# Linear attention beside weight products: the update of a pair's second state moved into the step that retrieves the next pair, its scaled keys and masked queries made a step ahead

## The chip, the cores and the metric

The program is one launch on one core of a Trainium2 chip. The metric is the time of that launch on the device in microseconds; for the kernel before, the median of three runs is given. Times inside the launch come from one further, profiled execution, and count from the start of its span.

## The reference, cut to what matters

One inference step of one decoder layer for a prompt of 256 tokens and for 8 sample sequences of 8 tokens. Everything is float32. The layer is feed-forward, token mixing, feed-forward; the token mixing has, beside an attention branch, a linear attention with a matrix state, 4 heads of 256 x 256 for each sample. For each sample and head it computes:

```
num   = wgt @ v + sc * (q @ C0)          # retrieval: queries on the old state
C_new = sT * C0 + sum_s e_s k_s v_s^T    # the state's update, an output
```

C0 is an input (8 samples x 4 heads x 256 KB) and C_new is an output of the same size. All 320 tokens (256 of the prompt, 64 of the samples) run through the same weight matrices.

## The kernel before, in words

The weight products take nearly all of TensorE's time. A float32 product is made of three matmuls in a rounded 32-bit format: weights and inputs are each split in a high and a low part. `run_job` goes through the weight matrices in chunks of 512 KB. For a chunk, SyncE issues the load into a tile `raw` (5 buffers), ScalarE makes the high part `hi` by a cast (L225), VectorE makes the low part `lo` by a subtraction (L226), three chunks ahead of their use (3 buffers each), and TensorE runs 24 matmuls into a PSUM tile `fg`.

All other work is written as Python generators ("background"), which `run_job` advances by one step between chunks; what a step issues stands in each engine's queue ahead of the chunk's matmuls, and behind the casts for the chunk three further on. There are lists `every`, `slow` (sample attention, 8 steps in 15 chunks), `even` and `odd`; a generator on `odd` gets one step every second chunk. The linear attention, `mlstm` (L995), is on `odd`. All loads and stores are issued by SyncE in one order, the order of the program. Each waits there for what it needs, and everything behind it waits with it. `later(fn, n)` puts a store at the start of the chunk n chunks on.

In `mlstm`, head h works through its 8 sample states in four pairs s4 = 0..3: the states of samples s4 and s4+4. Each pair takes two steps, here called A and B:

- Step A: `retrieve` (L1132), four matmuls of the masked queries `qm` on the two state tiles `C`; `state(h, s4)` (L1146), two matmuls of the scaled keys `ks` with the values `vs` into a PSUM tile `bg`, one VectorE operation that adds them to the state tile (L1153), and its store; `make_ks(h, s4 + 4)` (L1042), two ScalarE operations (L1047, L1048) and one on GpSimd (L1049). For s4 = 0 of the heads 1 to 3 also `rms_out(h - 1)` (L1200), three VectorE operations (L1202, L1204) and the store `hm_d<-hh`.
- Step B: `state(h, s4 + 4)`; `make_ks(h, s4 + 1)` and `make_qm(h, s4 + 1)` (two GpSimd operations, L1038) for the next pair; `load_cc`, two loads of 256 KB, for the pair after the next; and, for s4 = 2, `load_head(h + 1)`.

After the four pairs come `numer` (the prompt's part, and `load_vals`, the loads `vh<-vm_d` for the next head), `rms_in`, and a step with `rms_sum` and `update(h + 1)`, whose first matmuls read `vh`, and which loads the next head's second pair.

A state tile is one of nine buffers of the tag `m2`, shared with the head's other tiles. `ks` has two buffers, `qm` one, `bg` four, of which the retrieval holds one through the head.

Of the kernel before, what the change touches and what calls it, by code (L numbers as in the profile page):

```python
# [128 lines left out]
def decoder_kernel(tc, I, O, K):  # L129
# [10 lines left out]
    def dma(out, in_):  # L140
        nc.sync.dma_start(out, in_)

    def mm(out, a, b, start=True, stop=True, **kw):
        T.matmul(out, a, b, start=start, stop=stop, **kw)  # L144

    def bcast(ap, n, at=1):
        shape = list(ap.shape)
        shape.insert(at, n)
        idx = [slice(None)] * len(ap.shape)
        idx.insert(at, None)  # L150
        return ap[tuple(idx)].to_broadcast(shape)
# [6 lines left out]
    def later(fn, n=1):  # L158
        later_q.append([n, fn])
# [94 lines left out]
    def bg_tile():  # L254
        return pp.tile([128, 512], F32, tag="bg", bufs=4, name="bg")
# [119 lines left out]
    state = {}  # L375
# [135 lines left out]
    def mxt(shape, tag, bufs, name, dt=F32):  # L511
        return M["p"].tile(shape, dt, tag=tag, bufs=bufs, name=name)
# [407 lines left out]
    def qk_evac(ps, j):  # L920
# [35 lines left out]
        if M["qk"] == 2:  # L956
            spawn(mlstm(), odd)
# [37 lines left out]
    def mlstm():  # L995
# [12 lines left out]
        Cq = [None]  # L1008

        def load_head(h):  # L1010
            q, k, re = mp_tile("q"), mp_tile("k"), mp_tile("re")
            dma(q, qk_d[h].rearrange("p (a n) -> p a n", a=2))
            dma(k, qk_d[4 + h].rearrange("p (a n) -> p a n", a=2))
            dma(re, raw_ap(rows_d[:], h * 2 * NT, [[0, 128], [NT, 2], [1, NT]]))
            scb = mxt([128, 2 * NS], "scb", 1, "scb")
            dma(scb, sc_d[h:h + 1].to_broadcast([128, 2 * NS]))
            vq = m2_tile("vq")
            for g in range(2):
                dma(vq[:, g * 256:(g + 1) * 256], raw_ap(vm_d[:], (SEQ + 32 * g) * 1024 + h * 256,
                                                        [[0, 4], [1024, 32], [1, 256]]))  # L1020
            H[h] = {"q": q, "k": k, "re": re, "scb": scb, "vq": vq}

        def load_vals(h):
            v = m3_full("vh")
            G.memset(v[:, 0:2, 256:257], 1.0)
            dma(v[:, 0:2, 0:256], vm_d[0:SEQ, h * 256:(h + 1) * 256].rearrange("(t p) c -> p t c", p=128))
            dma(v[:, 2, 0:256], vm_d[NT - 128:NT, h * 256:(h + 1) * 256])
            H[h]["v"] = v

        def load_c(b, h):  # L1030
            t = m2_tile("C")
            dma(t.rearrange("p (k v) -> p k v", k=2), C0d[b, h].rearrange("(k p) v -> p k v", p=128))
            return t

        def make_qm(h, s4):
            qm = mxt([128, 2, 2, 32], "qm", 1, "qm")
            for kt in range(2):
                G.tensor_tensor(qm[:, kt], H[h]["qsc"][:, kt].rearrange("p (g c) -> p g c", g=2), bcast(qmk[:, s4], 2),  # L1038
                                op=OP.mult)
            H[h]["qm"] = qm  # L1040

        def make_ks(h, b):  # L1042
            d = H[h]
            ks = mxt([128, 256], "ks", 2, "ks", F32R)
            x, e = d["kr"][:, (b // 4) * 256:(b // 4 + 1) * 256], d["eb"][:, b:b + 1]
            kf = mxt([128, 256], "kf", 1, "kf")
            S.activation(ks, x, AF.Copy, scale=e)  # L1047
            S.activation(kf[64:128], x[64:128], AF.Copy, scale=e[64:128])  # L1048
            G.tensor_tensor(ks[64:128], kf[64:128], ks[64:128].bitcast(F32), op=OP.subtract)  # L1049
            d["ks"] = ks  # L1050

        def prep(h):
            d = H[h]
# [78 lines left out]
        def retrieve(h, s4):  # L1132
            d = H[h]
            if s4 == 0:
                d["ip"] = bg_tile()
            ip, qm = d["ip"], d["qm"]
            for kt in range(2):
                for n in range(2):
                    x = 32 * (kt * 2 + n)
                    mm(ip[x:x + 32, 0:256], qm[:, kt, n], Cq[0][n][:, kt * 256:(kt + 1) * 256], s4 == 0, s4 == 3,  # L1140
                       tile_position=(0, x))
            if s4 == 3:
                d["isb"] = mxt([128, 256], "isb", 1, "isb")
                S.copy(d["isb"], ip[:, 0:256])

        def state(h, b):  # L1146
            d = H[h]
            ks, vs_, t = d["ks"], d["vs"], Cq[0][b // 4]
            cu = bg_tile()
            for kt in range(2):  # L1150
                mm(cu[:, kt * 256:(kt + 1) * 256], ks[:, kt * 128:(kt + 1) * 128],
                   vs_[:, (b // 4) * 256:(b // 4 + 1) * 256])
            V.scalar_tensor_tensor(t, t, sTb[:, h * 8 + b:h * 8 + b + 1], cu, op0=OP.mult, op1=OP.add)  # L1153
            later(lambda: dma(C1d[b, h].rearrange("(k p) v -> p k v", p=128), t.rearrange("p (k v) -> p k v", k=2)))

        def numer(h):
            d = H[h]
            z, v, qn, re, isb = (d[x] for x in ("z", "v", "qn", "re", "isb"))
            A, B = bg_tile(), bg_tile()
            mm(B[:, 0:256], ones, z[:, 0:256], True, False)  # L1160
            mm(B[:, 128:256], ones, z[:, 256:384], False, True)
            mm(B[:, 256:320], ones, z[:, 384:448], True, False)
            mm(B[:, 256:320], ones, qn[:, 0], False, True)
            for vt in range(2):
                vs = slice(vt * 128, (vt + 1) * 128)
                o = vt * 256
                mm(A[:, o:o + 256], v[:, 0, vs], z[:, 0:256], True, False)
                mm(A[:, o + 128:o + 256], v[:, 1, vs], z[:, 256:384], False, True)
                c = 320 + 64 * vt
                mm(B[:, c:c + 64], v[:, 2, vs], z[:, 384:448], True, False)  # L1170
                mm(B[:, c:c + 64], isb[:, vs], sels, False, True)
            rd = re[:, 0]
            V.tensor_scalar(rd, B[:, 0:NT], -1.0, None, op0=OP.mult)
            V.tensor_tensor(rd, rd, B[:, 0:NT], op=OP.max)
            hh = mp_tile("hh")
            S.copy(hh[:, :, 0:SEQ], A.rearrange("p (a n) -> p a n", a=2))
            S.copy(hh[:, :, SEQ:NT], B[:, 320:448].rearrange("p (a n) -> p a n", a=2))
            V.tensor_tensor(rd, rd, re[:, 1], op=OP.max)
            V.reciprocal(rd, rd)
            V.tensor_tensor(hh, hh, bcast(rd, 2), op=OP.mult)  # L1180
            d["hh"] = hh
# [18 lines left out]
        def rms_out(h):  # L1200
            hh, rs, sg = (H[h][x] for x in ("hh", "rs", "sg"))
            V.tensor_tensor(hh, hh, bcast(rs, 2), op=OP.mult)  # L1202
            for m in range(2):
                V.scalar_tensor_tensor(hh[:, m], hh[:, m], gv[:, G_MN + 2 * h + m:G_MN + 2 * h + m + 1], sg[:, m],  # L1204
                                       op0=OP.mult, op1=OP.mult)
            later(lambda: dma(hm_d[h].rearrange("p (a n) -> p a n", a=2), hh), 2)

        seq = [(h, s4) for h in range(4) for s4 in range(4)]
        CC = {}

        def load_cc(i):
            if i < 16:
                h, s4 = seq[i]
                CC[i] = [load_c(s4, h), load_c(s4 + 4, h)]
# [12 lines left out]
        update(0)  # L1227
        load_cc(1)
        for h in range(4):
            for s4 in range(4):  # L1230
                yield
                Cq[0] = CC.pop(4 * h + s4)
                retrieve(h, s4)
                state(h, s4)
                make_ks(h, s4 + 4)
                if s4 == 0 and h:
                    rms_out(h - 1)
                yield
                state(h, s4 + 4)
                if s4 < 3:  # L1240
                    make_ks(h, s4 + 1)
                    make_qm(h, s4 + 1)
                    load_cc(4 * h + s4 + 2)
                if s4 == 2 and h < 3:
                    while M["qk"] < 2 * (h + 2):
                        yield
                    load_head(h + 1)
            yield
            numer(h)
            if h < 3:  # L1250
                load_vals(h + 1)
                prep(h + 1)
            while M["mo"] < h:
                yield
            yield
            rms_in(h)
            if h < 3:
                front(h + 1)
            yield
            rms_sum(h)  # L1260
            if h < 3:
                update(h + 1)
                load_cc(4 * h + 5)
# [495 lines left out]
```

## Time and profile before

| | |
|---|---|
| median of 3 runs | 2744.59 us (2739.4 to 2746.79) |
| the profiled execution's own time | 2745.51 us |
| its span | 2743.7 us |
| TensorE matmul busy | 2715.4 us (99%) |
| VectorE, ScalarE, GpSimd busy | 56%, 40%, 7% |
| time of the linear attention in the span | 1160 to 1580 us |
| DMA in 1200 to 1600 us | 320 GB/s |

The page gives shares over the whole span. `fg` are matmuls of the weight products, `bg` those of the background. A row of a timeline has the start, the duration, the engine, the line, the operation and its tiles; in brackets the idle time of the engine just before it and what ended that. A row of waits has who waited for whom, the sum, how often, and the longest. PE is TensorE, DVE VectorE, ACT ScalarE, POOL GpSimd, and SPq SyncE's queue, whose rows are the issues of DMAs, not their landing.

### The profile page before, as it was taken

How to read it: one execution, taken by the hardware profiler on the slowest of the kernel's cores; microseconds unless marked ns; L12 is line 12 of the kernel's file. 1: busy time of each engine (PE TensorE's matmuls, PEld its weight loads, DVE VectorE, ACT ScalarE, POOL GpSimd, SP SyncE). 2: the span in 40 equal slices, each digit the busy share in tenths (PEclk: the TensorE clock that was granted, in tenths of full speed). 3: DMA queues.
4: the chain of work that ended last, by engine and by line, in shares of the span. 5: the costliest groups of instructions: out<-in, count | busy, mean ns of one | idle time of the engine just before them, and what ended most of it. 6: DMA issues, size and time to landing. Idle time of an engine off the chain costs nothing.

```text
span 2743.7 us, 51211 instructions
## 1 busy us (share of the span) xinstructions
PE 2715.4 (99%) x21522; PEld 2670.7 (97%) x21522; DVE 1533.7 (56%) x1815; ACT 1105.5 (40%) x1379; POOL 181.3 (7%) x226
## 2 busy tenths in 40 slices
PE   9999999999999999999999999999999999999998
PEld 8999999999999999998899999999999999999998
DVE  6444444444446666786876765655444444444444
ACT  5333333333334443454544334444333333333344
POOL 0100000000000000111211100000000000000000
PEclk9999999999999999999999999999999999999999
DMA  6777777777756779999999997655555555555543
GB/s 216 239 226 249 225 237 230 225 235 232 240 186 189 235 193 307 299 321 282 337 335 330 324 298 232 201 190 158 165 162 161 159 165 162 161 156 170 162 151 116
DMA packets 521843, 607.56 MB, mean 221 GB/s; under 512 B 31948, under 2 KB 454396, under 8 KB 521588
## 3 DMA queue, kind: packets, MB, share of 16 engines
q1 hardware_dynamic: 520908, 602.77, 70.3%
q8 instruction: 168, 2.75, 0.4%
q10 hardware_dynamic: 704, 1.52, 0.2%
q14 instruction: 63, 0.52, 0.1%
HBM read 571.91 MB, written 82.61 MB: 239 GB/s over the span
## 4 chain that ended last, share of the span: by engine, by line
PE 50%; ACT 0%; POOLq 0%; POOL 0%; DVE 0%; issue 0%
PE fg L144 47%; PE bg L144 3%; PE bg L337 0%; POOLq L1755 0%; POOL Y L1719 0%; ACT hi L225 0%; ACT L1196 0%; ACT xn L1450 0%; DVE x L1445 0%; ACT sq L392 0%; DVE lo L226 0%; ACT re L1196 0%; DVE x L1469 0%; ACT sq L1470 0%; ACT rt L1704 0%
## 5 line engine op out<-in xcount | busy, mean ns | idle before, releaser
L226 DVE TENSOR_TENSOR lo<-raw,hi 128x1024 fp32r<-128x1024 f32 (+1 forms) x780 | 956.8, 1233 | 875.6 <-ACT hi L225 852.5
L144 PE MATMUL fg<-xh,hi 128*128 128x320 f32 x4240 | 1274.6, 302 | 0.5 <-ACT hi L225 0.5
L144 PE MATMUL fg<-xh,lo 128*128 128x320 f32 x4240 | 1265.0, 299 | 3.5 <-DVE lo L226 3.5
L144 PE MATMUL fg<-xl,hi 128*128 128x320 f32 x4240 | 1264.6, 299 | 0.0
L225 ACT CAST hi<-raw 128x1024 fp32r<-128x1024 f32 (+1 forms) x780 | 797.7, 1028 | 1071.1 <-PE fg L144 900.2
L144 PEld LDWEIGHTS fg<-xh,lo 128*128 128x128 f32 x4240 | 799.9, 189 | 4.6 <-DVE lo L226 4.5
L144 PEld LDWEIGHTS fg<-xh,hi 128*128 128x128 f32 x4240 | 799.8, 189 | 2.6 <-ACT hi L225 0.7
L144 PEld LDWEIGHTS fg<-xl,hi 128*128 128x128 f32 x4240 | 800.1, 189 | 0.7
L144 PE MATMUL fg<-hh,hi 128*128 128x320 f32 x1408 | 423.7, 301 | 0.0
L144 PE MATMUL fg<-hl,hi 128*128 128x320 f32 x1408 | 421.0, 299 | 0.0
L144 PE MATMUL fg<-hh,lo 128*128 128x320 f32 x1408 | 421.0, 299 | 0.0
L144 PEld LDWEIGHTS fg<-hh,hi 128*128 128x128 f32 x1408 | 266.1, 189 | 1.7 <-issue 1.6
L144 PEld LDWEIGHTS fg<-hl,hi 128*128 128x128 f32 x1408 | 266.1, 189 | 1.0 <-issue 1.0
L144 PEld LDWEIGHTS fg<-hh,lo 128*128 128x128 f32 x1408 | 266.1, 189 | 0.0
L466 POOL TENSOR_TENSOR gt<-gt,rstd 128x640 f32<-128x640 f32 x44 | 68.1, 1548 | 1789.2 <-ACT gt L465 1789.2
L144 PE MATMUL fg<-bh,hi 128*128 128x320 f32 x512 | 153.3, 299 | 0.0
L144 PE MATMUL fg<-bl,hi 128*128 128x320 f32 x512 | 153.1, 299 | 0.0
L144 PE MATMUL fg<-bh,lo 128*128 128x320 f32 x512 | 153.1, 299 | 0.0
L655 DVE STREAM_TRANSPOSE kd<-kraw 128x1024 f32<-128x1024 f32 x80 | 96.3, 1218 | 10.5 <-DMA kraw<-fk_d 10.5
L144 PEld LDWEIGHTS fg<-bh,hi 128*128 128x128 f32 x512 | 96.8, 189 | 0.2 <-issue 0.2
L144 PEld LDWEIGHTS fg<-bl,hi 128*128 128x128 f32 x512 | 96.8, 189 | 0.0
L144 PEld LDWEIGHTS fg<-bh,lo 128*128 128x128 f32 x512 | 96.8, 189 | 0.0
(301 smaller groups left out, 1371.7 us busy)
## 6 DMA issues: line engine op xcount, KB each, us to landing
raw<-in_w_in_dram SPq DMA_DIRECT2D x176, 512.0 KB
raw<-in_w_ffb_in_dram SPq DMA_DIRECT2D x176, 512.0 KB
raw<-in_w_ffa_in_dram SPq DMA_DIRECT2D x175, 512.0 KB
raw<-in_w_ffa_out_dram SPq DMA_DIRECT2D x80, 512.0 KB
raw<-in_w_ffb_out_dram SPq DMA_DIRECT2D x80, 512.0 KB
fk_d<-in_cache_k_dram SPq DMA_DIRECT2D x96, 256.0 KB
fv_d<-in_cache_v_dram SPq DMA_DIRECT2D x128, 192.0 KB
kraw<-fk_d SPq DMA_DIRECT2D x48, 512.0 KB
```

The source lines that it names most:

```text
L144: T.matmul(out, a, b, start=start, stop=stop, **kw)
L225: S.copy(hi[:, :nk], t[:, :nk])
L226: V.tensor_tensor(lo[:, :nk], t[:, :nk], hi[:, :nk].bitcast(F32), op=OP.subtract)
L466: G.tensor_tensor(gt, gt, bcast(rstd, 2), op=OP.mult)
L655: V.transpose(kd[:, 2 * pr:2 * pr + 2].rearrange("p a b -> p (a b)"), t.rearrange("p a b -> p (a b)"))
```

## The change

Step A of a pair now does nearly all: first the second state of the pair before (`state(h, s4 + 3)`, on that pair's tiles, which are kept as `Cp`), then the retrieval and the first state of this pair, both `make_ks`, `make_qm`, and the loads for the next pair. Step B is left with `rms_out` (s4 = 0) and `load_head` (s4 = 2); for s4 = 3 it does the last state. The number of steps, the instructions and the bytes are the same as before. The loads are issued by `load_cc(4 * h + s4 + 1)` in step A of s4 = 1, 2, 3, where `load_cc(4 * h + s4 + 2)` stood in step B of s4 = 0, 1, 2.

```diff
-            d["ks"] = ks
+            d.setdefault("ks", []).append(ks)
...
-        def state(h, b):
+        def state(h, b, pair):
             d = H[h]
-            ks, vs_, t = d["ks"], d["vs"], Cq[0][b // 4]
+            ks, vs_, t = d["ks"].pop(0), d["vs"], pair[b // 4]
...
-            for s4 in range(4):
-                yield
-                Cq[0] = CC.pop(4 * h + s4)
-                retrieve(h, s4)
-                state(h, s4)
-                make_ks(h, s4 + 4)
+            for s4 in range(5):
+                if s4 < 4:
+                    yield
+                if s4:
+                    state(h, s4 + 3, Cp)
+                if s4 < 4:
+                    Cp = Cq[0] = CC.pop(4 * h + s4)
+                    retrieve(h, s4)
+                    state(h, s4, Cp)
+                    make_ks(h, s4 + 4)
+                    if s4 < 3:
+                        make_ks(h, s4 + 1)
+                        make_qm(h, s4 + 1)
+                    if s4:
+                        load_cc(4 * h + s4 + 1)
+                    yield
                 if s4 == 0 and h:
                     rms_out(h - 1)
-                yield
-                state(h, s4 + 4)
-                if s4 < 3:
-                    make_ks(h, s4 + 1)
-                    make_qm(h, s4 + 1)
-                    load_cc(4 * h + s4 + 2)
```

On SyncE, at the first head, from its pair 0 to its pair 1; `C<-in_state_C` are the loads of pair 2, `raw` those of weights, `kraw` and `vt` those of the sample attention, `out_C_sample<-C` the stores of states (a piece of the difference):

```order
 L141 DMA kraw<-in_cache_k_dram 128x2x512
 L141 DMA vt<-in_cache_v_dram 128x2x512
-L141 DMA C<-in_state_C_dram 128x2x256 x2
 L141 DMA raw<-in_w_in_dram 128x4x256
 L141 DMA vt<-fv_d_117 96x1024
-L141 DMA out_C_sample_dram<-C 128x2x256
 L141 DMA raw<-in_w_in_dram 128x4x256
 L141 DMA vt<-fv_d_117 96x1024
 L141 DMA kraw<-in_cache_k_dram 128x2x512
-L141 DMA raw<-in_w_in_dram 128x4x256
-L141 DMA out_C_sample_dram<-C 128x2x256
+L141 DMA C<-in_state_C_dram 128x2x256 x2
```

The two loads stand five issues later, and one store of a state no longer stands between them and the weights.

On SyncE, at the end of the first head: `qs_d<-qS` writes the queries of the sample attention to memory, and the loads that read them, and behind these `vh<-vm_d`, follow the rows shown. Before:

```order
L141 DMA vm_d<-stage 128x2x256
L141 DMA vm_d<-stage 64x256
L141 DMA qs_d_91<-qS 128x256
L141 DMA raw<-in_w_in_dram 128x4x256
L141 DMA vt<-fv_d_118 96x1024
L141 DMA out_C_sample_dram<-C 128x2x256
L141 DMA kraw<-in_cache_k_dram 128x2x512
```

And now:

```order
L141 DMA vm_d<-stage 128x2x256
L141 DMA vm_d<-stage 64x256
L141 DMA C<-in_state_C_dram 128x2x256 x2
L141 DMA qs_d_91<-qS 128x256
L141 DMA raw<-in_w_in_dram 128x4x256
L141 DMA vt<-fv_d_118 96x1024
L141 DMA out_C_sample_dram<-C 128x2x256 x2
L141 DMA kraw<-in_cache_k_dram 128x2x512
```

The first pair of the second head is loaded just ahead of `qs_d<-qS`; in the kernel before those two loads stood ahead of `load_head`. One more store of a state stands behind `qs_d<-qS`, and one fewer ahead of it.

On VectorE, at the first pair of the second head: L1202 and L1204 are `rms_out`, L226 makes `lo`, L981 belongs to a gate's evacuation, L655 and L767 to L770 to the sample attention. Before:

```order
L1153 SCALAR_TENSOR_TENSOR C<-C,sTb,bg 128x512
L1202 TENSOR_TENSOR hh<-hh,re 128x640
L1204 SCALAR_TENSOR_TENSOR hh<-hh,gv,sgm 128x320 x2
L767 STREAM_TRANSPOSE sm<-sm 128x32
L768 TENSOR_REDUCE sm<-sm 128x8
L769 RECIPROCAL sm<-sm 128x8
L770 STREAM_TRANSPOSE sm<-sm 128x32
L655 STREAM_TRANSPOSE kd<-kraw 128x1024
L981 RECIPROCAL sg<-sg 128x320
L226 TENSOR_TENSOR lo<-raw,hi 128x1024
```

And now:

```order
L1153 SCALAR_TENSOR_TENSOR C<-C,sTb,bg 128x512
L767 STREAM_TRANSPOSE sm<-sm 128x32
L768 TENSOR_REDUCE sm<-sm 128x8
L769 RECIPROCAL sm<-sm 128x8
L770 STREAM_TRANSPOSE sm<-sm 128x32
L655 STREAM_TRANSPOSE kd<-kraw 128x1024
L981 RECIPROCAL sg<-sg 128x320
L226 TENSOR_TENSOR lo<-raw,hi 128x1024
L411 TENSOR_TENSOR mv<-fg,rstd 128x640
L226 TENSOR_TENSOR lo<-raw,hi 128x1024
L1202 TENSOR_TENSOR hh<-hh,re 128x640
L1204 SCALAR_TENSOR_TENSOR hh<-hh,gv,sgm 128x320 x2
```

The three operations of `rms_out` stand behind two weight subtractions that they stood ahead of.

## The prediction

> **What bounds the kernel now.** I read the page's totals, then the waits of TensorE, then its timeline around each wait, then the timelines of the engines that ended the waits. The totals of the page:
>
> ```profile
> span 2743.7 us, 51211 instructions
> PE 2715.4 (99%) x21522; PEld 2670.7 (97%) x21522; DVE 1533.7 (56%) x1815; ACT 1105.5 (40%) x1379; POOL 181.3 (7%) x226
> ```
>
> TensorE is busy for 99% of the span, and the change adds or removes no matmul. It moves work in the stretch of the linear attention alone. There it can gain only what TensorE waits, and lose only by making it wait more. The waits of TensorE from 1120 to 1620 us (for whom, sum, how often, longest):
>
> ```profile
> PE bg L144 <- DMA vh<-vm_d: 4.7, 1, 4.7
> PE fg L144 <- DVE lo L226: 2.1, 1, 2.1
> PE bg L144 <- POOL ks L1049: 1.2, 2, 0.9
> PE bg L144 <- ACT re L1196: 1.0, 1, 1.0
> PE bg L144 <- POOL qm L1038: 0.5, 1, 0.5
> ```
>
> These are 9.5 us in all, 0.35% of the span. A measurement of this kernel can tell about 0.3%, 8.2 us, from no change. So nearly every listed wait would have to go before a gain could be seen. Only new waits could make a visible loss.
>
> **Part by part.** The places, in TensorE's timeline:
>
> ```profile
> 1216.90 0.64 PE L144 MATMUL bg<-C,qm 128*32 128x256 f32 x8
> 1224.83 0.50 PE L144 MATMUL bg<-vs,ks 128*128 128x256 f32 x2 [0.34 <-POOL ks L1049]
> 1231.79 0.64 PE L144 MATMUL bg<-C,qm 128*32 128x256 f32 x8
> 1290.59 0.60 PE L337 MATMUL bg<-ident,krep 128*128 128x128 f32 x4
> 1295.91 3.77 PE L144 MATMUL bg<-vh,kw 128*128 128x257 f32 x8 [4.72 <-DMA vh<-vm_d]
> 1306.55 0.64 PE L144 MATMUL bg<-C,qm 128*32 128x256 f32 x8
> 1308.04 0.50 PE L144 MATMUL bg<-vs,ks 128*128 128x256 f32 x2 [0.85 <-POOL ks L1049]
> 1321.26 0.40 PE L144 MATMUL fg<-xh,lo 128*128 128x320 f32 x1 [2.10 <-DVE lo L226]
> 1360.21 0.91 PE L144 MATMUL bg<-C,qm 128*32 128x256 f32 x8 [0.55 <-POOL qm L1038]
> 1527.34 0.64 PE L144 MATMUL bg<-C,qm 128*32 128x256 f32 x8
> 1541.61 0.64 PE L144 MATMUL bg<-C,qm 128*32 128x256 f32 x8
> ```
>
> *Keys and queries.* The 0.34 us at 1224.83 is a step B that waits for keys made one step before. These keys are now made two steps, one pair, before their use, so the wait goes. The same holds for the masked queries at 1360.21: they come a step earlier, and 0.55 us go. The keys of a head's first pair (1308.04, 0.85 us) are not moved. In step A, ScalarE now writes both `ks` buffers, and must wait until this step's matmuls have read the old ones. That costs nothing: for the step at 1216.90 its `make_ks` ran at 1222.83, 6 us behind the matmuls, since it stands behind casts:
>
> ```profile
> 1222.83 0.51 ACT L1047 ACTIVATE ks<-kr,eb 128x256 fp32r<-128x256 f32 x1
> ```
>
> *The state's addition.* Step A issues two of VectorE's L1153 (742 ns each) and step B none. VectorE idles far more than that, 58.3 us from 1200 to 1590 us, in front of `lo` for the cast, so I cost this at nothing. Where that cover is gone, as at 1314 us, the cost is 0.74 us.
>
> ```profile
> L1153 DVE SCALAR_TENSOR_TENSOR C<-C,sTb,bg x32: 732/742/743, 1206.0 to 1571.1; 128x512 f32<-128x512 f32 x32
> DVE lo L226 <- ACT hi L225: 58.3, 42, 4.1
> ```
>
> *The loads of the states.* SyncE's queue around them:
>
> ```profile
> 1214.39 1.12 SPq L141 DMA_DIRECT2D C<-in_state_C_dram  x2
> 1223.27 0.37 SPq L141 DMA_DIRECT2D kraw<-in_cache_k_dram  x1
> 1224.85 0.37 SPq L141 DMA_DIRECT2D raw<-in_w_in_dram  x1
> 1231.50 1.96 SPq L141 DMA_DIRECT2D C<-in_state_C_dram  x2
> 1253.57 0.39 SPq L141 DMA_DIRECT2D raw<-in_w_in_dram  x1
> 1265.89 0.34 SPq L141 DMA_DIRECT2D qs_d<-qS  x1
> 1276.16 3.84 SPq L141 DMA_DIRECT2D q<-qs_d  x6
> 1290.44 1.17 SPq L141 DMA_DIRECT2D vh<-vm_d  x2
> 1349.96 0.37 SPq L141 DMA_DIRECT2D raw<-in_w_in_dram  x1
> 1534.61 0.37 SPq L141 DMA_DIRECT2D raw<-in_w_in_dram  x1
> ```
>
> The queue is never empty here. From 1253.57 to 1265.89 it issues eleven times in 12.32 us, one DMA per 1.12 us. The write `qs_d<-qS` issued at 1265.89 releases its reader at 1276.16; I take these 10.3 us as the time that any transfer needs from issue to landing in this stretch. The loads `vh<-vm_d`, issued from 1290.44, took 5.5 us until the wait ended at 1295.91, the lower bound; for the upper I choose a third more than 10.3, 13.6.
>
> The pair that is read at 1231.79 was issued at 1214.39 and is now issued after the `kraw` of 1223.27, just ahead of the `raw` of 1224.85. Three DMAs fewer stand ahead of it (the two loads themselves and one store), 3 x 1.12 = 3.4 us, so its two loads leave at about 1221.5 and 1222.6. The second lands at 1232.9. It is needed at 1231.45 (1231.79 less the 0.34 above). That is a new wait of 1.5 us; with 5.5 us of flight it is nothing, with 13.6 it is 4.8. It costs nothing in the end, for TensorE waits 4.72 us at 1295.91 for a transfer that doesn't hang on TensorE: what is lost or won before it is taken off that wait.
>
> For the other pairs the same count puts the issue 3.4 us ahead of the next `raw`. For 1360.21 that is 1346.6 and 1347.7, landing at 1358.0, against a need at 1359.66 (the 0.55 earlier): in time, and 1.6 us late with 13.6. For 1541.61 it is 1531.2 and 1532.4, landing at 1542.7: a new wait of 1.1 us (nothing to 4.4), and behind it no long wait takes it up. All other pairs land before they are needed by the same count.
>
> *The values of the next head.* The wait of 4.72 us is for `vh<-vm_d`. It stands in SyncE's queue behind the sixteen loads `q<-qs_d`, and these wait for `qs_d<-qS`, issued at 1265.89. One store of a state that stood ahead of that write now stands behind it, so it, its readers and `vh` come 1.12 us earlier. With the 1.5 us lost before and the 0.34 won, the wait would shrink from 4.72 to 4.72 - 1.1 - 1.5 + 0.34 = 2.5 us. What TensorE's end gains is only the 1.1 us.
>
> The clock has a part in this wait (stretch, length, busy times, granted clock, DMA share, GB/s):
>
> ```profile
> 1291.19:1293.57 2.38, 0.00 (x1) 0.00 (x0) 2.24 (x6) 1.01 (x3) 0.00 (x0) 1.00 1.00 317
> 1293.57:1295.91 2.34, 0.00 (x0) 0.03 (x1) 2.24 (x8) 1.55 (x4) 0.00 (x0) 0.50 0.91 256
> 1295.91:1300.40 4.49, 4.49 (x12) 3.75 (x13) 1.56 (x2) 4.42 (x5) 0.00 (x0) 0.50 1.06 387
> ```
>
> The last matmul ended at 1291.19. The granted clock fell to 0.5 after 2.38 us and stayed there until 1300.40, so 4.49 us of matmuls went at half rate, a loss of 2.25 us. The wait of 2.10 us at 1321.26 had no such drop. A wait of 2.5 us lies between: the drop may go. I give nothing for it, because 1308.04 takes it up: there TensorE waits for keys that ScalarE makes behind a chain that VectorE and a load end, not TensorE:
>
> ```profile
> 1286.12 1.05 ACT L225 CAST hi<-raw 128x1024 fp32r<-128x1024 f32 x1 [2.84 <-DMA raw<-in_w_in_dram]
> 1295.76 1.28 ACT L949 ACT_TABLE_LOAD   x1 [0.79 <-DVE y L945]
> 1306.61 0.50 ACT L1048 ACTIVATE kf<-kr,eb 64x256 f32<-64x256 f32 x1
> ```
>
> If TensorE comes there 2.25 us sooner, its wait of 0.85 grows to 3.1. This chain has the same 1.1 us from the earlier queue, so the 1.1 stands either way.
>
> [...]
>
> *The output's rescaling.* `rms_out` of the first head stands in VectorE's queue ahead of two `lo`:
>
> ```profile
> 1314.24 0.82 DVE L1202 TENSOR_TENSOR hh<-hh,re 128x640 f32<-128x640 f32 x1
> 1315.10 1.01 DVE L1204 SCALAR_TENSOR_TENSOR hh<-hh,gv,sgm 128x320 f32<-128x320 f32 x2
> ```
>
> It takes 0.82 + 1.01 = 1.83 us, and it now comes behind them. VectorE works without a pause up to the `lo` that ends the wait of 2.10 us at 1321.26. So this wait shrinks by 1.83 to 0.3 us. In its new place `rms_out` has idle time of VectorE in front of a later `lo` as cover; without that it would give the 1.83 back. The other two `rms_out` have no wait near them.
>
> *The sum* for the profiled execution of 2745.51 us: -1.1 (`vh`) - 1.83 (`lo`) - 0.55 (`qm`) + 1.1 (a late state) = -2.4, which is 2743.1. The median of the runs lies 0.92 below the profiled one, so 2742.2, said as 2742. The bounds: without the late state -3.5. With 4.4 for it in place of 1.1, and with the drop of the clock moved onto a wait that nothing takes up (+2.25), and 1.6 for the state at 1360.21, +4.8.
>
> **The rivals.**
>
> *The waits only move.* The `lo` at 1321.26 stands in a queue of VectorE that is full for 20 us, and the extra L1153 and the later `rms_out` only hit the next `lo`; the 1.1 us of the `vh` is eaten by the same jammed queue. What is left is the 0.55. The time is 2744. For it speaks that bytes and instructions are the same; against it that VectorE has idle time. Chance 0.18.
>
> *Faster.* If the queue's order moves `vh` by more than one place in time, for example because the loads ahead of it land sooner when the state loads don't compete, the whole wait of 4.72 goes, and with it the drop. With -1.83, -0.55 and up to the 0.85 at 1308.04: -7.1 to -8.0, so 2736.5 from the median. Against it: the DMA engines are at a share of 0.91 to 1.06 in the rows above. Chance 0.10.
>
> *Slower: the states come late.* The loads are now asked for one pair ahead and not one and a half, and the queue runs behind the program. In the kernel before, the pair issued by the first head's second step B is the one of 1231.50: it left when TensorE had been at step B (1224.83) for 6.7 us, the second 8.6. With 10.3 us of flight it is there 17.0 to 18.9 us after the step that asks. The window from one retrieval to the next is 14.27 us from 1527.34 to 1541.61 and 14.89 from 1216.90 to 1231.79. A pair would then be late by 2.1 to 4.6 us (17.0 - 14.89, 18.9 - 14.27) at each such place, and a wait over 2.38 us brings the half clock, 2.25 us more. Two to three places at 4 to 5 us are +8 to +14; with the gains, about +10, so 2755. It decides where lag plus flight is above 14.3. For it speaks the full queue; against it that the order of the queue, counted above, puts the loads only five issues later and not a whole pair. Chance 0.10.
>
> [...]
>
> **Chances.** The forecast has 0.62. The slower rival lies above +8.2 us, and 0.02 of the forecast I put there too, for several late states at once. The faster one ends at -8.0, close to the bound, and most of its 0.10, 0.08, I count as faster, to be careful. The rest lies within. Faster 0.08, same 0.80, slower 0.12. The range goes from the faster rival's 2736 to 2750, which takes in the forecast's +4.8 and half of the way to the slower one.
>
> **What would show it.** Right, if in the new profile the waits for `qm` at the second head's pair and for the first step's `ks` are gone, the wait for `vh` is 2 to 3 us, the wait for the `lo` behind the second head's first pair is under 0.5, and `bg` waits for a `C` load once or twice, by 1 to 2 us. The slices before and behind the wait for `vh` show whether the clock still drops. Wrong, if waits for `C` loads add up to over 5 us, if the wait for `vh` is under 1 or over 4 us, if a new wait for `lo` stands a chunk or two behind the old one, or if `ks` at 1308.04 has become the longest wait.

## The result and the profile after

The changed kernel takes 2750.99 us (median of 21 runs, 2745.64 to 2755.05), the kernel before 2744.59 (21 runs, 2739.4 to 2753.48). The ratio is 1.0020, with a 95% interval of 1.0014 to 1.0027: slower by a fifth of a per cent, some 6 us. The forecast was 2742; the range ended at 2750. The profiled execution took 2752.04 us.

The page's totals of the changed kernel: TensorE's work is the same, and it is still at 99%.

```profile
span 2750.3 us, 51203 instructions
PE 2717.4 (99%) x21522; PEld 2673.7 (97%) x21522; DVE 1530.9 (56%) x1815; ACT 1105.8 (40%) x1379; POOL 182.6 (7%) x226
```

The waits of TensorE from 1120 to 1640 us in the changed kernel:

```profile
PE bg L144 <- DMA vh<-vm_d: 4.4, 2, 3.0
PE bg L144 <- DMA C<-in_state_C_dram: 3.1, 1, 3.1
PE bg L337 <- ACT stage L543: 3.0, 1, 3.0
PE bg L144 <- POOL ks L1049: 2.5, 1, 2.5
PE bg L337 <- DVE C L1153: 0.4, 1, 0.4
```

They add up to 13.4 us against 9.5, +3.9. The old waits for `lo`, `re` and `qm` are gone, as is the one for the first `ks`. There are four new or longer ones. TensorE's timeline of the changed kernel has their places:

```profile
1233.26 1.60 PE L144 MATMUL bg<-C,qm 128*32 128x256 f32 x8 [3.09 <-DMA C<-in_state_C_dram]
1296.06 1.98 PE L144 MATMUL bg<-vh,kw 128*128 128x257 f32 x8 [1.37 <-DMA vh<-vm_d]
1307.62 0.50 PE L144 MATMUL bg<-vs,ks 128*128 128x256 f32 x2 [2.49 <-POOL ks L1049]
1327.83 0.44 PE L337 MATMUL bg<-ident,mv 128*128 128x128 f32 x2 [2.99 <-ACT stage L543]
1363.93 0.64 PE L144 MATMUL bg<-C,qm 128*32 128x256 f32 x8
1503.82 3.41 PE L144 MATMUL bg<-vh,kw 128*128 128x257 f32 x8 [3.03 <-DMA vh<-vm_d]
```

The waits are half of it. Behind each of the four longest the clock halves. The stretches of the changed kernel around them (stretch, length, busy times of PE, PEld, DVE, ACT and POOL, granted clock, DMA share, GB/s):

```profile
1230.25:1233.66 3.41, 0.40 (x2) 0.14 (x2) 3.41 (x3) 1.55 (x3) 1.67 (x1) 1.00 1.09 351
1233.66:1237.07 3.41, 3.41 (x16) 2.48 (x16) 2.64 (x4) 1.01 (x2) 0.34 (x1) 0.50 1.08 404
1305.34:1308.75 3.41, 1.13 (x9) 1.14 (x10) 3.04 (x9) 3.37 (x7) 1.84 (x2) 1.00 1.06 365
1308.75:1312.17 3.42, 3.42 (x15) 3.42 (x14) 3.42 (x4) 2.42 (x6) 1.86 (x4) 0.50 1.11 319
1325.82:1329.23 3.41, 1.41 (x11) 1.41 (x12) 1.96 (x4) 1.09 (x2) 2.12 (x4) 1.00 1.05 373
1329.23:1332.65 3.42, 3.42 (x15) 3.42 (x15) 0.00 (x0) 0.00 (x0) 0.00 (x0) 0.50 1.07 390
1499.90:1503.31 3.41, 0.89 (x6) 0.50 (x4) 2.00 (x2) 2.90 (x4) 0.00 (x0) 1.00 1.06 313
1503.31:1506.73 3.42, 2.91 (x7) 2.39 (x8) 0.16 (x1) 2.55 (x4) 0.00 (x0) 0.50 1.07 398
```

TensorE works 3.41 + 3.42 + 3.42 + 2.91 = 13.16 us at clock 0.50. In the first of these stretches the weight matmuls start 0.27 us apart (1235.64, 1235.91), behind it 0.14 us (1237.16, 1237.30), so half of the 13.16 us is lost, 6.6 us by my estimate. Before, it was 4.49 us, 2.25 lost. That is +4.3 us. With +3.9 of waits it makes +8.2. The span grew by 6.6. What is missing is mostly the start: the same group of matmuls has these rows (min, median and max ns, first and last start) before, and then now:

```profile
L144 PE MATMUL bg<-vh,kw x32: 377/382/767, 1188.8 to 1500.3; 128*128 128x257 f32 x32
```

```profile
L144 PE MATMUL bg<-vh,kw x32: 377/382/767, 1187.7 to 1506.8; 128*128 128x257 f32 x32
```

The changed execution is 1.1 us ahead when the linear attention begins, ahead of anything that the change moved, and 6.5 us behind at the last head's update. It stays so to the end.

### The profile page after: what moved, and what is told of

It is laid out like the page before. It is cut to its first block, busy times and chain, and to the rows that moved or that the text cites. A ratio compares the mean times of both kernels' runs of the same rounds, so it can differ in the third digit from the quotient of the medians.

```text
span 2750.3 us, 51203 instructions
## 1 busy us (share of the span) xinstructions
PE 2717.4 (99%) x21522; PEld 2673.7 (97%) x21522; DVE 1530.9 (56%) x1815; ACT 1105.8 (40%) x1379; POOL 182.6 (7%) x226
## 4 chain that ended last, share of the span: by engine, by line
PE 92%; DMA 4%; DVE 2%; ACT 1%; issue 0%; SPq 0%; POOL 0%; POOLq 0%; ACTq 0%; DVEq 0%
PE fg L144 87%; PE bg L144 5%; PE bg L337 1%; DMA raw<-in_w_in_dram 1%; DMA vt<-fv_d 1%; DVE lo L226 1%; DMA kraw<-fk_d 1%; DMA C<-in_state_C_dram 0%; DMA vh<-vm_d 0%; DMA kraw<-in_cache_k_dram 0%; ACT hi L225 0%; SPq L141 0%; DMA xl<-in_x_prompt_dram 0%; DMA gate_d<-sg 0%; DVE kd L655 0%
## 5 line engine op out<-in xcount | busy, mean ns | idle before, releaser
L226 DVE TENSOR_TENSOR lo<-raw,hi 128x1024 fp32r<-128x1024 f32 (+1 forms) x780 | 955.5, 1232 | 883.5 <-ACT hi L225 849.4
L655 DVE STREAM_TRANSPOSE kd<-kraw 128x1024 f32<-128x1024 f32 x80 | 96.3, 1218 | 4.8 <-DMA kraw<-fk_d 4.8
```

The costliest lines, as they stand in the source:

```text
L226: V.tensor_tensor(lo[:, :nk], t[:, :nk], hi[:, :nk].bitcast(F32), op=OP.subtract)
L655: V.transpose(kd[:, 2 * pr:2 * pr + 2].rearrange("p a b -> p (a b)"), t.rearrange("p a b -> p (a b)"))
```

## The experiments

All ratios are to the kernel before on the same chip, 11 runs against 33. Their intervals are some 0.1% to either side, 2.5 us, so a smaller difference between two runs tells nothing.

| run | ratio | 95% interval |
|---|---|---|
| loads_back | 1.0022 | 1.0013 to 1.0031 |
| state_back | 1.0000 | 0.9992 to 1.0009 |
| both_back | 1.0001 | 0.9992 to 1.0010 |
| loads_only | 1.0009 | 1.0000 to 1.0018 |
| stage_later | 1.0012 | 1.0003 to 1.0021 |
| stores_later | 1.0010 | 1.0002 to 1.0019 |
| filler | 1.0001 | 0.9992 to 1.0010 |
| before_vals | 0.9999 | 0.9990 to 1.0008 |
| after_vals | 1.0018 | 1.0008 to 1.0029 |
| keys_vals | 1.0014 | 1.0005 to 1.0023 |
| last_vals | 0.9981 | 0.9972 to 0.9990 |
| before_lv | 0.9995 | 0.9986 to 1.0004 |
| last_vals_stores | 0.9990 | 0.9981 to 0.9998 |
| stage_last_vals | 1.0000 | 0.9991 to 1.0008 |
| state_back_lv | 1.0002 | 0.9991 to 1.0012 |
| loads_back_lv | 0.9997 | 0.9988 to 1.0006 |

### Which part of the change costs

The loads alone put back:

```diff
-                    if s4:
-                        load_cc(4 * h + s4 + 1)
                     yield
+                    if s4 < 3:
+                        load_cc(4 * h + s4 + 2)
```

> The changed kernel with only the state loads put back to step B, for the pair after the next. Theory: the +6.4 us have two roots, the loads that come later in SyncE's queue (the wait of 3.09 us for a C load at 1233, the wait of 3.03 us for the last head's values at 1504) and the two states of one step, which take two of the four bg tiles at once (the wait of 2.99 us for the stage copy L543 at 1328); each wait brings a stretch at half clock worth up to 1.7 us. Then the C wait and the last head's vh wait go here, the L543 wait stays at 2 to 3 us with its half-clock stretch, and the time is 2746 to 2748. Rival 'only the loads', all else following from TensorE's lateness: the L543 wait goes too, 2742 to 2744. Rival 'only the two states in one step': no change from the changed kernel, 2750 to 2752.

The second state alone put back:

```diff
-            for s4 in range(5):
...
-                if s4:
-                    state(h, s4 + 3, Cp)
+            for s4 in range(4):
...
                     yield
+                    state(h, s4 + 4, Cp)
```

> The changed kernel with only the second state put back to step B of its own pair; keys, queries, loads and the output's rescaling as changed. Theory of two roots: the wait for the stage copy L543 goes, the waits for a C load (near 3 us) and for the last head's values (near 3 us) stay, 2746 to 2748. Rival 'only the loads': all waits stay, 2750 to 2752. Rival 'only the two states in one step': 2742 to 2744.

Both put back, so that only keys, queries and `rms_out` are moved:

> The kernel before with only the keys and queries made a step ahead and the output's rescaling in step B (second state and loads as before). Theory and both rivals: none of the new waits; the prediction's terms for the lo (1.83) and the qm (0.55) stand alone, 2744.6 - 2.4 = 2742, if nothing takes them up. If the keys made ahead have a price of their own (ScalarE then makes two ks in one step, behind which the stage copy stands), 2745 or more and a wait for L543 of over 1 us.

The kernel before with the loads alone moved (`load_cc(4 * h + s4 + 1)` into step A of pairs 1 to 3):

> The kernel before with only the loads changed (asked in step A of pairs 1 to 3 for the next pair). Theory of two roots: a wait for a C load of 1.5 to 3 us that the wait for the first vh pays back, and the last head's vh late by 2 to 3 us with a half-clock stretch; 2747 to 2749, no wait for L543. Rival 'only the loads': 2750 to 2752. Rival 'only the two states': 2744 to 2745.

The move of the second state carries the loss: with the loads back it stays whole (1.0022), with the state back it is gone (1.0000), and the two intervals don't touch. My theory of two equal roots fell with loads_back, where the rival "only the two states" held. On the kernel before, the moved loads alone cost 0.1% (1.0000 to 1.0018), as the theory had it, and TensorE waits 2.2 us for the last head's `vh`; state_back has the same moved loads and is no slower than both_back, so a price of the loads is not clear of the noise here. The waits of loads_back:

```profile
PE bg L144 <- ACT re L1196: 3.5, 1, 3.5
PE bg L337 <- ACT stage L543: 3.0, 1, 3.0
PE bg L144 <- POOL ks L1049: 2.5, 1, 2.5
PE bg L144 <- DMA vh<-vm_d: 2.4, 1, 2.4
```

The wait for the stage copy is the same 3.0 us, and the last head's update now waits for `re` (3.5 us) in place of `vh`. The waits of state_back:

```profile
PE bg L144 <- DMA vh<-vm_d: 3.4, 1, 3.4
PE bg L144 <- POOL ks L1049: 3.3, 1, 3.3
PE bg L144 <- DVE y L945: 2.5, 1, 2.5
PE bg L144 <- DMA C<-in_state_C_dram: 0.9, 1, 0.9
```

No wait for the stage copy. Yet both_back, which should have earned the 2.4 us of the prediction, is no faster than before (1.0001). Its waits:

```profile
PE bg L144 <- DMA vh<-vm_d: 5.0, 2, 3.9
PE bg L144 <- POOL ks L1049: 2.7, 1, 2.7
```

The waits for `lo` and `qm` are gone there, and a wait of 3.9 us for the last head's values stands in their place.

### What the second state meets

This is the place in the changed kernel, first TensorE's timeline, then ScalarE's, then VectorE's:

```profile
1323.00 0.40 PE L144 MATMUL bg<-vs,ks 128*128 128x256 f32 x2
1323.33 0.64 PE L144 MATMUL bg<-C,qm 128*32 128x256 f32 x8
1323.90 0.50 PE L144 MATMUL bg<-vs,ks 128*128 128x256 f32 x2
1324.24 0.60 PE L337 MATMUL bg<-ident,mv 128*128 128x128 f32 x4
```

```profile
1325.08 0.51 ACT L1047 ACTIVATE ks<-kr,eb 128x256 fp32r<-128x256 f32 x1
1326.66 0.50 ACT L1048 ACTIVATE kf<-kr,eb 64x256 f32<-64x256 f32 x1 [1.07 <-POOL ks L1049]
1327.18 0.59 ACT L543 COPY stage<-bg 128x512 f32<-128x512 f32 x1
```

```profile
1325.95 1.40 DVE L1153 SCALAR_TENSOR_TENSOR C<-C,sTb,bg 128x512 f32<-128x512 f32 x2
```

Of the four `bg` tiles the retrieval holds one through the head. The two states now take two at once, the first transposes of the V job the fourth. Its second transposes find none free. The states' tiles come free when VectorE has added them, the first at 1326.69 (742 ns after its start), the second at 1327.35, the transposes' own first tile when ScalarE has copied it, at 1327.77; TensorE goes on at 1327.83. So by the profile it waits for the copy, and not for either addition; loads_back and after_vals show the same, 3.0 and 2.3 us, both ended by this copy. The shortage of tiles itself is read from the kernel's text, not from a row. Two `make_ks` in a row add to it: they share one buffer `kf`, so the second waits 1.07 us for GpSimd, and the copy stands behind it. The next run moves only the transposes:

```diff
         yield
         yield
+        if h == 3:
+            yield
         tok_major(v, vm_d[0:SEQ, ...
```

> The changed kernel with the transposes of the last V job (L543, L544) one chunk later, so that they don't meet the two states of a step. Theory of the tiles: the second state's price is the wait of 2.99 us at 1328 for a free bg tile with its half-clock stretch, and through it the late values of the last head; without it no wait for L543, the wait for the last vh shrinks by 2 us or more, and the time is 2746 to 2748. Rival 'the states' own lateness': adding and storing the second state a step later delays the queue by itself; the wait for L543 goes but the time stays at 2750 to 2752.

The wait for L543 is gone, and the ratio falls from 1.0020 to 1.0012. That is the direction of the tile theory, but the two intervals overlap (1.0014 to 1.0027 and 1.0003 to 1.0021), the time lies between the two expectations, and the wait for the last head's values did not shrink, it grew to 5.6 us:

```profile
PE bg L144 <- DMA vh<-vm_d: 8.5, 2, 5.6
```

So these values are late without that wait too. The change also stores each second state a step later. The next run does only that, on state_back:

```diff
-            later(lambda: dma(C1d[b, h]...))
+            later(lambda: dma(C1d[b, h]...), 3 if b > 3 else 1)
```

> The run state_back (second state in its own step B) with only the stores of the second states queued two chunks, one step, later. Theory that late stores crowd the queue in front of the last head's values: vh of the last head lands 1.5 to 2.5 us later than in state_back and TensorE's wait of 3.38 us there grows by as much; the time 1 to 3 us above state_back. Rival 'the queue is full anyway, its order doesn't matter': no change, 2745 to 2747.

1.0010 against 1.0000: the later stores may cost about 0.1%, which the two intervals don't settle. The wait for the last head's `vh` is 3.9 us against 3.4; it grew by 0.5 us, less than the 1.5 to 2.5 expected.

### The values as the second limit

`load_vals` was put into step A of a head's last pair, on three kernels: the one before, the changed one, and both_back (this is keys_vals):

```diff
+                if s4 == 3 and h < 3:
+                    load_vals(h + 1)
                 yield
...
             if h < 3:
-                load_vals(h + 1)
                 prep(h + 1)
```

> The kernel before with only the values loaded early. Theory: the wait of 4.72 us at 1296 and its half clock go in part (ks at 1308 is held by its own chain), the prediction's terms for lo and qm stay unearned; 2741 to 2744. If the last head's vh was no limit in this kernel and ks takes up everything: 2745 to 2747.

> The changed kernel with the next head's values loaded in step A of the last pair, some ten DMAs earlier in SyncE's queue. Theory that the values' landing collects what the stretch loses (the DMAs are the second limit): the waits for vh at 1296 and 1504 go, with one or two half-clock stretches; 2745 to 2747. Rival 'another chain is right behind' (re L1196, ks L1049): the wait is named otherwise and the time stays within 2 us of 2751.

> The run with keys, queries and rescaling moved but states and loads as before, and with the values loaded early. That run was 6 to 7 us ahead at 1360 us and lost it at a wait of 3.9 us for the last head's vh with a half-clock stretch. Theory of the second limit at vh: the gain of 5 to 7 us now stays, 2739 to 2742. Rival 'another chain is right behind': 2744 to 2747, with a wait for re L1196 or C in the place.

The waits for `vh` went, but nothing was gained. At the second head TensorE now waits for `qm` or `re` and then for `ks`, 3.4 to 3.9 us each, at 1303 and 1308. The rival "another chain is right behind" held there: this is the chain of ScalarE that the prediction had named. keys_vals, at 2750.85 us, is slower than its rival's 2744 to 2747 as well; its profile has one more wait, of 2.9 us at 1426, ended by `cs` L969. So the last head's values alone were loaded early, on both_back:

```diff
+                    if s4 == 3 and h == 2:
+                        load_vals(3)
                     yield
...
-                load_vals(h + 1)
+                if h != 2:
+                    load_vals(h + 1)
```

> The run both_back (keys, queries and rescaling moved; states and loads as before) with the values of the last head alone loaded early. Theory of the second limit: what both_back gained by 1360 us it lost at its wait of 3.9 us for the last head's vh with 6.8 us of half clock; without that wait the gain stays: 2740 to 2743, no PE wait over 2 us after 1400. Rival 'another chain is right behind at that place': a wait of 2 us or more for re L1196 or a C load near 1500 to 1550, and 2745 to 2748.

0.9981 (0.9972 to 0.9990), 2740.33 us against 2745.88 in that comparison: faster than both kernels, and as expected. Its waits have none in the last head:

```profile
PE bg L144 <- DMA vh<-vm_d: 4.0, 1, 4.0
PE bg L144 <- ACT re L1196: 1.0, 1, 1.0
PE bg L144 <- POOL ks L1049: 1.0, 1, 1.0
PE fg L144 <- DVE lo L226: 0.3, 1, 0.3
```

The same edit on the kernel before:

> The kernel before with only the last head's values early. The values' wait was not there before (its vh landed some 1.4 us ahead of need), so if the gain of last_vals is that of lo and qm, now kept: ratio 0.9995 to 1.0005. If the early values gain by themselves: 0.998 to 0.999.

0.9995: nothing that can be told. The early values alone gain nothing, nor do the moved keys, queries and `rms_out` alone (both_back, 1.0001); together they gain 0.2%. So the moved work brings the gain, and the early values are what lets it stand. Then the same edit on the changed parts, to see what each costs once the values don't collect it:

> The run stage_later (the changed kernel without the meeting of the V job's transposes with the two states) with the values of the last head loaded early as well. It waited 5.57 us for them with 6.8 us of half clock. Theory: the changed kernel's whole loss is the tile wait and the late values, so this is as fast as last_vals within 2 us, 2740 to 2744. Rival: the second state costs elsewhere too: 2747 or more.

> The run state_back (second state in its own step; keys, queries, rescaling and loads as changed) with the last head's values loaded early. If the changed loads cost nothing when no late value collects: as last_vals, ratio 0.998, 2740 to 2742. If the loads are the open half: ratio 1.000, 2745 to 2746.

> The second state a step later as changed, loads as before, the V job's transposes a chunk later, the last head's values early. If the state's move itself (matmuls, addition, store) is the open half: ratio 1.000, 2745 to 2746. If it was the loads: 0.998, 2740 to 2742.

> The run last_vals with the stores of the second states queued two chunks later. If the later stores cost by more than the last head's values: ratio 0.9995 to 1.0005, 2744 to 2746, with a new wait for a DMA somewhere. If they cost only there: 0.998, 2740 to 2742.

Against last_vals the changed loads (state_back_lv) lose 0.2%, the moved state (loads_back_lv) 0.16%, the later stores 0.1%, and all together (stage_last_vals) 0.2%. They don't add up, the intervals are 0.1% to either side, and last_vals was measured on another chip than the three with one part each. state_back_lv and loads_back_lv came out at the slower of their two expectations, the other two between theirs. In the profiled executions state_back_lv and loads_back_lv wait longer for `ks` at the second head, 3.4 and 3.0 us against 1.0 in last_vals. Beside that, state_back_lv waits 3.2 us for two `C` loads, and loads_back_lv 3.9 us at the second head's update, which the profile puts down to `y` L947; it no longer waits there for `vh`, as last_vals did for 4.0. That the loads and the moved state each take the gain of last_vals away is shown, the latter by little more than the intervals; that the later stores do is not, and how the prices divide stays open.

### The half clock

Matmuls of constants into a tile that is written over afterwards, five ahead of the second head's first state and eight ahead of the last head's update, on both_back:

```diff
+            if h == 3:
+                for _ in range(8):
+                    mm(cu[0][:, 0:256], ones, cm[:, 0:256])
...
+            if h == 1 and b == 0:
+                for _ in range(5):
+                    mm(cu[:, 0:256], ones, cm[:, 0:256])
```

> The run both_back with 5 matmuls of constants ahead of the second head's first state and 8 ahead of the last head's update, about 1.2 and 2 us of TensorE work in its waits of 2.67 and 3.9 us; they are written over. Theory that each wait of over some 2 us costs a stretch of half clock on top: no half-clock stretch at 1302 and at 1493, 3 us faster than both_back (2743 to 2744). Rival 'the half clock is hidden, since a date set by the DMAs follows': the stretches go, the time stays at 2746 to 2747, and a wait for a DMA grows.

At the last head's update these matmuls stand in TensorE's timeline as

```profile
1492.43 3.62 PE L144 MATMUL bg<-mixc,ones 128*128 128x256 f32 x16
```

The eight products are sixteen matmuls there and took 3.62 us, not the 2 us that I had expected. The stretches around both places in filler, and then in both_back:

```profile
1280.00:1340.00 60.00, 56.59 (x545) 50.96 (x533) 45.31 (x75) 32.91 (x51) 15.09 (x19) 1.00 1.02 329
1490.00:1520.00 30.00, 30.00 (x308) 27.24 (x308) 16.02 (x28) 13.78 (x21) 4.11 (x6) 1.00 1.00 315
```

```profile
1280.00:1340.00 60.00, 56.26 (x526) 51.64 (x515) 45.45 (x75) 34.43 (x53) 14.27 (x19) 0.97 1.03 333
1490.00:1520.00 30.00, 26.10 (x269) 23.06 (x268) 12.74 (x24) 13.88 (x21) 4.11 (x6) 0.89 0.89 281
```

The half clock is gone (1.00 against 0.97 and 0.89). The ratio stays at 1.0001, and the medians, 2745.94 and 2746.89, differ by less than they can tell. No gain of 3 us (0.11%) shows, but one of that size is not excluded by the two intervals. Whether the half clock was hidden behind a DMA stays open too: the added matmuls fill the waits of 2.67 and 3.90 us nearly whole, so a longer wait for a DMA would not have been seen there.

## Why the prediction was wrong

**Keys and queries:** right. The waits at 1224.83 and 1360.21 are gone; the row at 1363.93 has no wait. The claim that two `make_ks` in one step cost ScalarE nothing failed: I looked at the buffers of `ks` and not at the single `kf`, which costs 1.07 us ahead of a copy that TensorE waits for.

**The state's addition, "at nothing":** this is the step that failed. I asked only whether VectorE had time for two additions in a row. The price is the tiles that the two states hold. The `bg` tiles stood in my own description of the kernel, four with one held, and I did not count them through the new step. The wait is 2.99 us, with 1.7 us of half clock behind it (3.42 / 2). That the moved state carries the loss is shown (loads_back 1.0022, state_back 1.0000). That this wait is the whole of its price is not: stage_later has no such wait, and still takes 1.0012.

**The loads of the states:** right in kind. The late pair at 1231 was forecast at 1.5 us within 0 to 4.8; it is 3.09. The size is that of one execution: after_vals, stage_later and stage_last_vals run the same program up to there and waited 0.3, 0.6 and 0.3 us. It was paid back as forecast: TensorE reached the next head's values late, waited only 1.37 us for them in place of 4.72 (2.5 was forecast), and went on at 1296.06 against 1295.91. The late pair at 1541.61 did not come, for TensorE was late itself; at 1548.14 nothing waits. Where TensorE is earlier it comes: loads_only waits 1.1 us for this pair, as forecast, and after_vals 2.5.

**The values of the next head:** wrong twice. At the second head they were to come 1.1 us earlier; against a start that is 1.1 us earlier in this execution they came at the same time, so by the program they are a little over 1 us later. And I costed the wait where the profile had one, and not the place where it had none. The last head's update ran without a wait before:

```profile
1498.71 1.98 PE L144 MATMUL bg<-vh,kw 128*128 128x257 f32 x8
```

Its values' loads leave SyncE's queue 4.66 us later now; the rows are of before and of the changed kernel:

```profile
1487.26 2.20 SPq L141 DMA_DIRECT2D vh<-vm_d  x2
```

```profile
1491.92 2.30 SPq L141 DMA_DIRECT2D vh<-vm_d  x2
```

With TensorE on time, or ahead, this transfer is the limit: it made waits of 3.03 us here, 3.4 in state_back, 3.9 in both_back, 5.6 in stage_later. It is why the terms for `lo` and `qm`, whose waits went as forecast, earned nothing in both_back until last_vals took it away.

**The clock:** I asked only whether the old half clock would go. It went, and the wait at 1307.62 grew from 0.85 to 2.49 us as I had said (up to 3.1). But four waits now bring a stretch each, and that is +4.3 us of the profiled execution. The prediction gave the half clock a price only in the bounds and in the slower rival, which let every wait over 2.38 us bring it; the last section has waits of 2.5 and 2.9 us that no half clock followed, and one of 2.1 us that it did follow.

**The rivals:** the slower one had the sign, with the wrong mechanism: it put all on the late `C` loads, of which one came and was paid back. "The waits only move" is nearest to what happened in both_back.

## What to carry to other kernels

When work is regrouped into fewer, larger steps, count through the new step each rotating buffer that its operations hold until another engine is done, PSUM tiles first; a free engine doesn't make a free tile (here a wait of 2.99 us). Before a removed wait is booked as a gain, look for the next transfer that is only just in time further on, since it collects the gain as a new wait (3.9 us for the last head's values in both_back). And look at what follows a wait of TensorE: here waits of 2.5 to 4.7 us were followed by 1.5 to 2.3 us lost at half clock, though taking the half clock away in filler gained nothing that could be told.

## What the runs showed of the hardware

In the changed kernel the four longest waits of TensorE, 2.49 to 3.09 us, were each followed by a stretch of 3.41 or 3.42 us at clock 0.50. In the 3.41 us just ahead of these stretches TensorE had worked for 0.40, 1.13, 1.41 and 0.89 us. These rows, of last_vals_stores, state_back and stage_later, are from the second head:

```profile
1291.11:1294.52 3.41, 1.39 (x7) 1.25 (x8) 3.31 (x8) 2.62 (x5) 0.00 (x0) 1.00 0.89 260
1294.52:1297.93 3.41, 3.41 (x13) 3.23 (x12) 0.89 (x2) 3.34 (x5) 0.00 (x0) 0.50 1.07 399
```

```profile
1288.76:1292.17 3.41, 2.75 (x20) 2.31 (x18) 3.13 (x10) 1.26 (x4) 0.00 (x0) 1.00 0.98 305
1292.17:1295.58 3.41, 1.58 (x7) 1.44 (x8) 3.41 (x8) 2.61 (x4) 0.00 (x0) 1.00 0.96 302
1295.58:1299.00 3.42, 3.42 (x26) 3.38 (x25) 0.25 (x1) 3.36 (x5) 0.00 (x0) 1.00 1.06 389
```

```profile
1288.45:1291.86 3.41, 2.24 (x16) 1.79 (x14) 3.18 (x9) 1.98 (x5) 0.00 (x0) 1.00 1.00 308
1291.86:1295.27 3.41, 1.63 (x9) 1.47 (x9) 2.94 (x6) 2.60 (x4) 0.00 (x0) 1.00 0.99 310
1295.27:1298.69 3.42, 3.42 (x26) 3.39 (x25) 0.00 (x0) 3.39 (x4) 0.68 (x1) 1.00 1.07 388
```

In last_vals_stores a wait of 2.1 us was followed by a stretch at 0.50. In state_back a wait of 2.5 us, and in stage_later one of 2.9 us (8.5 less 5.6), were not: their rows are all at 1.00. So in these runs the length of a wait alone doesn't say whether half clock follows. What decides it was not tried.
